# Fixed places for the factors, an earlier norm and a fourth activation tile in a two-layer trunk

## The chip, the cores and the metric

The kernel runs on one core of a Trainium2 chip. A core has five engines with a queue each, which run independently and wait for each other by semaphores: TensorE (PE, matrix products into PSUM; PEld is its loading of weights), VectorE (DVE), ScalarE (ACT), GpSimd (POOL, which can't reach PSUM) and SyncE (SP, which here issues loads). The metric is the device time of one execution in microseconds (us), as a median of several runs.

## What is computed

One inference step of two layers on 1056 tokens (1024 of a prompt, 32 of a running stream) with 1024 features, in float32. Layer 0 mixes tokens with a gated linear recurrence (HGRN2), layer 1 with a short causal convolution; after each comes an MLP.

```
for i in range(DEPTH):                       # DEPTH = 2
    a = rmsnorm(h, norm_mix[i])
    y = hgrn2_mixer(a, ...) if i == 0 else short_conv_mixer(a, ...)
    h = h + y
    m = rmsnorm(h, norm_mlp[i])
    h = h + jnp.square(jax.nn.relu(m @ w_up[i])) @ w_down[i]   # 1024 -> 4096 -> 1024
return rmsnorm(h, norm_final), states
```

## The kernel before

Activations lie transposed: a tile is 128 features by 1056 tokens, and `hT` are the eight tiles of `h`. Each float32 product is made of three matmuls of rounded operands: the low half of the weight by the high half of the activation, high by low, and high by high. A split (`part`, lines 597 to 604) is an ACT cast (the high half) and a DVE subtraction (the low half).

An MLP (`mlp`, line 844) goes through the 4096 hidden features in 16 chunks of 256. `up(c)` makes a chunk's two hidden tiles `u`, `sums(c)` turns them into seven factors, and `down(c, 0)` and `down(c, 1)` multiply these into the two halves of `hT`. Both products use a scheme of Strassen's kind: sums of blocks of the weights (made on GpSimd, line 756) times factors of the activations, which are named B11, B22, Q1, Q2, T3, B21 and T4 (`xsums`, line 765, in which the sums overwrite `u` in place).

A `down` has seven steps of 12 matmuls (`STEPS`, line 744), 84 in all, that read B11, Q1, Q2, B22, T3, B21 and T4 in this order. After each step its result is added to `hT`: by DVE (line 915), or, for the first and the last step, by an ACT copy into a tile `st` (two buffers, line 912) and a GpSimd add (line 913). An `up` has eleven products (`PAIR`, line 811): seven with a factor, of 12 matmuls each, and four with plain rows of the input, of 24 each, 180 matmuls in all. Products with the same letter there add up in the same PSUM tile; one that is read in between must be read before the next adds to it. The first `up` of an MLP takes them in the order `LATE` (line 814) and calls `nrm.scale` ahead of product 10, which is the tenth in that order; `scale` (line 701) spreads the sum of squares with matmuls (line 707) and computes 1/rms on DVE in a chain of whole-tile operations (lines 143 to 149). The ends of the first `up` (relu, times 1/rms, square) run after its products.

The stages follow in the text as up(0), sums(0), up(1), down(0,0), down(0,1), sums(1), up(2), down(1,0), down(1,1), and so on. The weights of a stage are loaded and split two stages ahead in the text. Factors, norm tiles and others share one rotation of seven buffers (`zt`, line 627); `u` tiles have three (`ut`, line 630); a weight's halves have six buffers each (`wb`, line 619); PSUM has four tiles of two banks (`pb`, line 622).

No order is written by hand here. A scheduler at compile time simulates the program and puts into each engine's queue, of the instructions that are ready in its simulation, the one that stands first in the text. A tile that takes over a buffer waits for the readers of the one before. On the chip each queue then goes strictly in order. Pools opened after others are closed lie over the closed ones' memory: at line 619 those of the HGRN stage have just been closed, with `fp` (activations) ahead of `ws` (weights).

Of the kernel before, what the change touches and what calls it, by code (L numbers as in the profile page):

```python
# [16 lines left out]
P = 128  # L17
D = 1024
KT = D // P
NTOK = 1056  # L20
# [15 lines left out]
def trunk_kernel(  # L36
# [579 lines left out]
    fp_cm.__exit__(None, None, None)  # L616


    wb = ctx.enter_context(tc.tile_pool(name="wb", bufs=6, reuse_waits="tile"))
    hb = ctx.enter_context(tc.tile_pool(name="hb", bufs=1, reuse_waits="tile"))  # L620
    mp = ctx.enter_context(tc.tile_pool(name="mp", bufs=1, reuse_waits="tile"))
    pb = ctx.enter_context(tc.tile_pool(name="pb", bufs=4, space=PSUM, reuse_waits="tile"))

    def ht(name):
        return hb.tile([P, NTOK], F32, tag="h", name=name, bufs=8)

    def zt(name, dtype=F32):
        return hb.tile([P, NTOK], dtype, tag="z", name=name, bufs=7)

    def ut(name, dtype=F32):  # L630
        return hb.tile([P, NTOK + 4], dtype, tag="u", name=name, bufs=3)[:, :NTOK]

    work["dg"] = ut

# [77 lines left out]

    def out_proj(W, first, xsrc, vcol):

        nrm = Norm(zt)
        X = None
        for m in range(KT):
            wt = wrow(W[m])
            if first:
                hT[m] = ht(f"hT{m}")  # L720
                nc.gpsimd.dma_start(out=hT[m], in_=x_t[m * P : (m + 1) * P, :])
            _, pss = trio()
            mm_groups(pss, wt, xsrc, m in (0, KT - 1))
            for g in range(3):
                sl, n = gsl(g)
                nc.vector.tensor_tensor(hT[m][:, sl], hT[m][:, sl], pss[g][:, :n], op=ALU.add)
            nrm.add(m)
            if m in (3, 5):
                X = hsums(m // 2 - 1, X, vcol)
        X["rows"] = [parts(hT[k], vec[:, vcol + k : vcol + k + 1]) for k in range(4, KT)]  # L730
        return nrm, X
# [56 lines left out]

    def hsums(q, X, vcol):

        t = [zt("hs") for j in range(2)]
        for j in range(2):
            m = 2 * q + j
            nc.scalar.activation(t[j], hT[m], AF.Copy, scale=vec[:, vcol + m : vcol + m + 1])
        new = xt if q else lambda f: xt(f) if f == "T4" else et(f, F32R)
        Y = xsums(*t, new)
        return {f: (X[f] if X else []) + [Y[f]] for f in Y}
# [46 lines left out]
    def mlp(layer, nrm, on_final, last, X):  # L844
# [3 lines left out]
        def up(c):  # L848
            def run(w):
                u = [ut("u") for j in range(2)]  # L850
                left = {b: list(READ.values()).count(b) for b in READ.values()}
                made = set()

                def read(what, ps):
                    i, h = b = READ[what]
                    sl = slice(h * HALF, (h + 1) * HALF)
                    d = u[i][:, sl]
                    op0 = ALU.min if i else ALU.max
                    left[b] -= 1
                    src = d  # L860
                    if b in made:
                        nc.vector.tensor_tensor(q2(d), q2(d), ps, op=ALU.add)
                    elif left[b] or c == 0:
                        nc.scalar.copy(q2(d), ps)
                    else:
                        src = ps
                    made.add(b)
                    if not left[b]:
                        r = lambda: nrm.r[:, sl]

                        def end():
                            if src is d:
                                nc.vector.scalar_tensor_tensor(d, d, 0.0, r(), op0=op0, op1=ALU.mult)
                            else:
                                nc.vector.scalar_tensor_tensor(q2(d), src, 0.0, q2(r()), op0=op0, op1=ALU.mult)
                            if c:
                                nc.scalar.activation(d, d, AF.Square)
                            else:
                                nc.vector.tensor_tensor(d, d, d, op=ALU.mult)

                        later.append(end) if c == 0 else end()

                later = []
                if c:
                    mm_pair(w, X, read)
                else:
                    mm_pair(w, X, read, LATE, {10: nrm.scale})
                for f in later:
                    f()
                U[c] = u  # L890

            return lambda: wpair(Wu[c]), run

        def sums(c):
            Z[c] = xsums(*U.pop(c), lambda f: zt(f, F32R))

        def down(c, b):
            def run(w):
                x = Z[c]
                ps = [{}, {}]  # L900
                for i, (bank, f, g, start) in enumerate(STEPS):
                    for p in range(2):
                        if start:
                            ps[p][bank] = pt()
                        t = ps[p][bank]
                        mm_half(t, w(f, p), x[g], start, True)
                        v = t[:, :, :QT]
                        r, h, op = TO[i]
                        d = hT[4 * b + 2 * p + r][:, h * HALF : (h + 1) * HALF]
                        if i in (0, 6):  # L910
                            st = mp.tile([P, HALF], F32, tag="st", name="st", bufs=2)
                            nc.scalar.copy(q2(st), v)  # L912
                            nc.gpsimd.tensor_tensor(d, d, st, op=op)  # L913
                        else:
                            nc.vector.tensor_tensor(q2(d), q2(d), v, op=op)  # L915

            return lambda: wsums(Wd[c, b]), run
# [18 lines left out]
            return lambda: wblocks(Wd[NFC - 1, b]), run  # L936

        G = []

        def gsplit(u, new):  # L940
            h, l = [new(t, F32R) for t in ("gh", "gl")]
# [46 lines left out]
        stages.append(up(n))  # L988
        if last:
            stages += [down(n - 1, 0), down(n - 1, 1)]  # L990
            stages.append(lambda: [gsplit(u, zt) for u in U[n]])
            stages.append(up(n + 1))
            stages.append(lambda: [gsplit(U[n + 1][0], zt), gsplit(U[n + 1][1], lambda t, d: (zt if t == "gh" else ut)(t, d))])
            stages.append(groups())
        else:
            stages.append(down(n - 1, 0))
# [24 lines left out]
    with tc.tile_pool(name="cv", bufs=1) as cv:  # L1021
# [2 lines left out]
        ys = []  # L1024
        for m in range(KT):
            wts = [wrow(wg_cu_conv[2 * m + j]) for j in range(2)]
            z = hb.tile([P, NTOK + 4], F32, tag="u", name="z", bufs=3)
            zp = lambda g: [(z[:, 2 + GROUPS[g][0] : 2 + min(NPR, sum(GROUPS[g]))], 0, min(NPR, sum(GROUPS[g])) - GROUPS[g][0])] + (
                [(z[:, NPR + 4 : NTOK + 4], NPR - GROUPS[g][0], NTOK - GROUPS[g][0])] if g == 2 else [])
            nc.gpsimd.memset(z[:, 0:2], 0.0)  # L1030
# [28 lines left out]
            nc.scalar.activation(ct, z[:, 0:L], AF.Copy, scale=w(0))  # L1059
            nc.vector.scalar_tensor_tensor(ct, z[:, 1 : 1 + L], w(1), ct, op0=ALU.mult, op1=ALU.add)  # L1060
            nc.vector.scalar_tensor_tensor(ct, z[:, 2 : 2 + L], w(2), ct, op0=ALU.mult, op1=ALU.add)
            y = (zt if m < 7 else ut)(f"y{m}")
            nc.vector.tensor_tensor(y[:, :NPR], ct[:, :NPR], r[:, :NPR], op=ALU.mult)
            nc.vector.tensor_tensor(y[:, NPR:], ct[:, NPR + 2 :], r[:, NPR:], op=ALU.mult)
            ys.append(y)
# [15 lines left out]
    def fin1(g, m):  # L1081
# [20 lines left out]
        if (g, m) == (2, KT - 1):  # L1102
            final_scale(g)
            for k0 in range(0, KT, 2):
                o = zt("o")[:, : 2 * n].rearrange("p (k c) -> p k c", k=2)
                for k in range(2):
                    final_mul(g, k0 + k, nc.gpsimd if k0 + k in (2, 5) else nc.vector, o[:, k])
                nc.sync.dma_start(out=y_t[k0 * P : (k0 + 2) * P, sl].rearrange("(k p) c -> p k c", p=P), in_=o)
# [109 lines left out]
```

## Time and profile before

| what | value |
|---|---|
| median of 3 runs | 2489.42 us (2489.13 to 2491.89) |
| profiled execution | 2489.7 us |
| its span, first to last instruction | 2488.0 us |
| mean granted TensorE clock | 0.988 |
| busy: PE, DVE, ACT, POOL | 96%, 71%, 37%, 32% |

Times in rows are microseconds from the span's start. Where a row ends in square brackets, the engine was idle for that long before the instruction, until the named releaser was done. Layer 0's MLP runs from about 628 to 1370, layer 1's from about 1735 to 2488.

### The profile page before, as it was taken

The page shows a single profiled execution, that of the slowest core. Times are in us where ns is not written, and L with a number is a line of the kernel's source. Part 1 is how long each engine was busy: PE and PEld are TensorE (multiplying, and loading weights), DVE is VectorE, ACT ScalarE, POOL GpSimd, SP SyncE. Part 2 cuts the span into 40 slices and gives each one's busy share as a digit, 9 for nine tenths or more (in the row PEclk, how much of TensorE's full clock was granted, in tenths as well). Part 3 has the DMA queues.
Part 4 walks back from the last instruction along what each step waited for, and adds up shares of the span by engine and source line. Part 5 has one row for each costly group of instructions (what it writes and reads, how often), then busy time and mean ns, then how long its engine had stood idle before and what let it go on. Part 6 is the DMA issues. An engine that isn't in the chain of part 4 may idle for free. (4 is left out here: it accounts for less than half of the span.)

```text
span 2488.0 us, 42845 instructions
## 1 busy us (share of the span) xinstructions
PE 2392.9 (96%) x17700; PEld 2339.4 (94%) x17700; DVE 1769.9 (71%) x2842; ACT 917.8 (37%) x1671; POOL 792.2 (32%) x920
## 2 busy tenths in 40 slices
PE   8999999979799999999999999999899999999998
PEld 8999999979799999999999999999799999999997
DVE  8775757553888788887888633345888887888865
ACT  5121212133344444444445111134244444444444
POOL 2110101002245454444545000002254544545433
PEclk9999999989899999999999999999899999999999
DMA  4101010031011111111111111110111111111111
GB/s 148 38 30 46 24 52 21 13 123 43 26 52 52 43 43 52 52 52 44 43 52 52 51 43 51 43 45 33 35 52 43 52 52 43 52 43 52 52 52 70
DMA packets 35779, 122.23 MB, mean 49 GB/s; under 512 B 4336, under 2 KB 7552, under 8 KB 35584
## 3 DMA queue, kind: packets, MB, share of 16 engines
q1 hardware_dynamic: 33632, 113.58, 14.4%
q0 software_dynamic: 1952, 5.92, 0.6%
q8 instruction: 139, 2.28, 0.4%
q14 instruction: 56, 0.46, 0.1%
HBM read 114.09 MB, written 5.39 MB: 48 GB/s over the span
## 5 line engine op out<-in xcount | busy, mean ns | idle before, releaser
L600 ACT CAST whi<-raw 128x512 fp32r<-128x512 f32 (+1 forms) x476 | 275.9, 580 | 756.3 <-PE pb L117 290.9
L756 POOL TENSOR_TENSOR raw<-raw 128x256 f32<-128x256 f32 x360 | 307.1, 853 | 538.5 <-DVE wlo L601 523.8
L601 DVE TENSOR_TENSOR wlo<-raw,whi 128x512 fp32r<-128x512 f32 (+1 forms) x476 | 327.9, 690 | 142.3 <-ACT whi L600 140.6
L915 DVE TENSOR_TENSOR hT<-hT,pb 128x528 f32<-128x528 f32 x580 | 389.4, 697 | 54.2 <-PE pb L806 49.1
L913 POOL TENSOR_TENSOR hT<-hT,st 128x528 f32<-128x528 f32 x232 | 339.4, 1474 | 194.4 <-ACT st L912 194.4
L806 PE MATMUL pb<-B,whi 128*128 128x264 f32 x2160 | 353.9, 286 | 5.5 <-DVE B L601 5.5
L115 PE MATMUL pb<-xh,wlo 128*128 128x384 f32 (+1 forms) x960 | 312.4, 325 | 9.3 <-DVE wlo L601 9.3
L117 PE MATMUL pb<-xh,whi 128*128 128x384 f32 (+1 forms) x960 | 311.0, 324 | 0.0
L116 PE MATMUL pb<-xl,whi 128*128 128x384 f32 (+1 forms) x960 | 309.9, 323 | 0.8 <-DVE xl L604 0.8
L806 PEld LDWEIGHTS pb<-B,whi 128*128 128x128 f32 x2160 | 301.7, 190 | 5.9 <-DVE B L601 5.9
L806 PE MATMUL pb<-B,wlo 128*128 128x264 f32 x1080 | 224.4, 289 | 41.0 <-DVE hT L915 21.7
L806 PE MATMUL pb<-T,whi 128*128 128x264 f32 x1440 | 234.8, 285 | 0.0
L806 PE MATMUL pb<-Q,whi 128*128 128x264 f32 x1440 | 233.8, 284 | 0.0
L806 PEld LDWEIGHTS pb<-B,wlo 128*128 128x128 f32 x1080 | 168.4, 190 | 48.4 <-DVE hT L915 28.0
L806 PE MATMUL pb<-xh,wlo 128*128 128x264 f32 x1024 | 210.1, 286 | 0.0
L806 PE MATMUL pb<-xh,whi 128*128 128x264 f32 x1024 | 209.1, 285 | 0.0
L806 PE MATMUL pb<-xl,whi 128*128 128x264 f32 x1024 | 208.6, 285 | 0.0
L806 PEld LDWEIGHTS pb<-T,whi 128*128 128x128 f32 x1440 | 200.3, 189 | 0.0
L806 PEld LDWEIGHTS pb<-Q,whi 128*128 128x128 f32 x1440 | 199.2, 188 | 0.0
L115 PEld LDWEIGHTS pb<-xh,wlo 128*128 128x128 f32 x960 | 181.1, 189 | 9.7 <-DVE wlo L601 9.4
L115 PE MATMUL pj<-xh,wlo 128*128 128x384 f32 (+1 forms) x536 | 176.6, 330 | 6.5 <-ACT xh L192 6.5
L116 PEld LDWEIGHTS pb<-xl,whi 128*128 128x128 f32 x960 | 180.9, 188 | 1.2 <-DVE xl L604 1.2
(265 smaller groups left out, 4875.7 us busy)
## 6 DMA issues: line engine op xcount, KB each, us to landing
raw<-in_wg_up_dram SPq DMA_DIRECT2D x64, 512.0 KB, 3.5
raw<-in_wg_down_dram SPq DMA_DIRECT2D x64, 512.0 KB, 3.5
raw<-in_wg_in_hgrn_dram SPq DMA_DIRECT2D x31, 512.0 KB, 4.0
raw<-in_wg_cu_conv_dram SPq DMA_DIRECT2D x16, 512.0 KB, 3.6
xk<-in_x_t_dram SPq DMA_DIRECT2D x8, 528.0 KB, 8.3
hT<-in_x_t_dram POOLq DMA_DIRECT2D x8, 528.0 KB, 9.3
raw<-in_wg_out_hgrn_dram SPq DMA_DIRECT2D x8, 512.0 KB, 4.9
raw<-in_wg_b_conv_dram SPq DMA_DIRECT2D x8, 512.0 KB, 3.6
```

The source lines that it names most:

```text
L115: nc.tensor.matmul(ps, wlo, ah, start=start, stop=False)
L116: nc.tensor.matmul(ps, whi, al, start=False, stop=False)
L117: nc.tensor.matmul(ps, whi, ah, start=False, stop=stop)
L600: nc.scalar.copy(h, src)
L601: nc.vector.tensor_tensor(l, src, h.bitcast(F32), op=ALU.subtract)
L756: nc.gpsimd.tensor_tensor(t(d), t(d), t(o), op=ALU.add)
L806: nc.tensor.matmul(ps[:, q, :QT], w, half(v, q), start=start and n == 0, stop=stop and n == 2, skip_group_check=True)
L913: nc.gpsimd.tensor_tensor(d, d, st, op=op)
L915: nc.vector.tensor_tensor(q2(d), q2(d), v, op=op)
```

## The change

The factors of a chunk no longer rotate. Each has a fixed place, a buffer of its own, and takes in the next chunk the place that another factor had (`AFTER`): B11 that of T4, T4 that of B11, B22 that of B21, B21 that of T3, T3 that of Q1, Q1 that of B22; Q2 stays. Norm tiles, `hsums`, the conv stage's `y`, the last chunks' halves and the output tiles get fixed places as well. In the first `up`, `nrm.scale` is called ahead of product 2, the sixth in `LATE`, and so after five products. There are four `u` tiles, four `st` buffers and seven buffers for each weight half; the SBUF for them comes from GpSimd's DMA scratch, 4096 instead of the default 16384 bytes of a partition. The pool `hb` is opened ahead of `wb`.

```diff
-    wb = ctx.enter_context(tc.tile_pool(name="wb", bufs=6, reuse_waits="tile"))
     hb = ctx.enter_context(tc.tile_pool(name="hb", bufs=1, reuse_waits="tile"))
+    wb = ctx.enter_context(tc.tile_pool(name="wb", bufs=7, reuse_waits="tile"))
...
-    def zt(name, dtype=F32):
-        return hb.tile([P, NTOK], dtype, tag="z", name=name, bufs=7)
+    def zt(i, name, dtype=F32):
+        return hb.tile([P, NTOK], dtype, tag=f"z{i}", name=name, bufs=1)

     def ut(name, dtype=F32):
-        return hb.tile([P, NTOK + 4], dtype, tag="u", name=name, bufs=3)[:, :NTOK]
+        return hb.tile([P, NTOK + 4], dtype, tag="u", name=name, bufs=4)[:, :NTOK]
...
-        nrm = Norm(zt)
+        sqs = iter((0, 1, 2, 1, 2, 1, 2, 1, 2))
+        nrm = Norm(lambda name: zt(next(sqs), name))
...
-        t = [zt("hs") for j in range(2)]
+        t = [zt(3 + 2 * q + j, "hs") for j in range(2)]
...
-                    mm_pair(w, X, read, LATE, {10: nrm.scale})
+                    mm_pair(w, X, read, LATE, {2: nrm.scale})
...
+        AFTER = {"B11": "T4", "B22": "B21", "B21": "T3", "Q1": "B22", "Q2": "Q2", "T3": "Q1", "T4": "B11"}
+        place = {f: i for i, f in enumerate(AFTER)}
+
         def sums(c):
-            Z[c] = xsums(*U.pop(c), lambda f: zt(f, F32R))
+            Z[c] = xsums(*U.pop(c), lambda f: zt(place[f], f, F32R))
+            place.update({f: place[AFTER[f]] for f in AFTER})
...
-                            st = mp.tile([P, HALF], F32, tag="st", name="st", bufs=2)
+                            st = mp.tile([P, HALF], F32, tag="st", name="st", bufs=4)
...
+        gi = iter(range(8))
+
+        def gz(name, dtype):
+            i = next(gi)
+            return zt(i, name, dtype) if i < 7 else ut(name, dtype)
...
-            z = hb.tile([P, NTOK + 4], F32, tag="u", name="z", bufs=3)
+            z = hb.tile([P, NTOK + 4], F32, tag="u", name="z", bufs=4)
...
-            y = (zt if m < 7 else ut)(f"y{m}")
+            y = zt(m, f"y{m}") if m < 7 else ut(f"y{m}")
...
-                o = zt("o")[:, : 2 * n].rearrange("p (k c) -> p k c", k=2)
+                o = zt(k0 // 2, "o")[:, : 2 * n].rearrange("p (k c) -> p k c", k=2)
...
-    nc = _bacc.Bacc("TRN2", target_bir_lowering=False, num_devices=1)
+    nc = _bacc.Bacc("TRN2", target_bir_lowering=False, num_devices=1, dynamic_dma_scratch_size=4096)
```

## Rows read from the trace of the kernel before

**Rows 1.** The page's first part: busy time, share of the span, instructions.
```profile
PE 2392.9 (96%) x17700; PEld 2339.4 (94%) x17700; DVE 1769.9 (71%) x2842; ACT 917.8 (37%) x1671; POOL 792.2 (32%) x920
```

**Rows 2.** PE's waits, whole span: waiter <- releaser: us in total, times, longest.
```profile
PE pb L806 <- DVE hT L915: 31.1, 57, 1.8
PE pb L806 <- ACT u L864: 21.0, 4, 9.5
PE pb L115 <- DVE wlo L601: 9.3, 1, 9.3
```

**Rows 3.** Busy us by stretch: one chunk's first `down`, second `down`, and an `up`.
```profile
1044.37:1054.59 10.22, 10.22 (x86) 10.22 (x85) 8.66 (x14) 4.38 (x8) 5.45 (x6) 1.00 0.08 30
1054.59:1066.80 12.21, 11.20 (x87) 10.48 (x86) 10.53 (x16) 5.76 (x11) 8.95 (x9) 1.00 0.19 51
1022.45:1044.37 21.92, 21.92 (x182) 21.92 (x181) 17.24 (x25) 10.32 (x18) 6.90 (x6) 1.00 0.19 56
```
The columns of this view are the stretch, its length, the busy time of PE, PEld, DVE, ACT and POOL with their instructions, the granted clock, the DMA share and GB/s.

**Rows 4.** PE's waits in the steady stretches 700 to 1300 and 1800 to 2360.
```profile
PE pb L806 <- DVE hT L915: 14.4, 28, 0.8
...
PE pb L806 <- DVE hT L915: 13.3, 26, 0.8
```

**Rows 5.** In order of time, a second `down`: ACT, then DVE (start, us, instruction).
```profile
1057.62 0.60 ACT L912 COPY st<-pb 128x528 f32<-128x528 f32 x1 [0.87 <-POOL hT L913]
1058.12 1.17 ACT L600 CAST B<-u 128x528 fp32r<-128x528 f32 x2
...
1057.00 0.70 DVE L915 TENSOR_TENSOR hT<-hT,pb 128x528 f32<-128x528 f32 x1 [0.60 <-PE pb L806]
1058.79 1.34 DVE L601 TENSOR_TENSOR B<-u,B 128x528 fp32r<-128x528 f32 x1 [1.08 <-ACT B L600]
1060.06 2.53 DVE L915 TENSOR_TENSOR hT<-hT,pb 128x528 f32<-128x528 f32 x4
```

**Rows 6.** Busy us by stretch: `up(1)` from first to last matmul, layers 0 and 1.
```profile
653.23:690.47 37.24, 25.01 (x188) 24.49 (x187) 31.65 (x40) 11.87 (x20) 8.48 (x5) 0.82 0.09 27
1759.92:1798.32 38.40, 26.21 (x188) 25.69 (x187) 31.64 (x40) 11.85 (x20) 8.47 (x5) 0.78 0.09 28
```

**Rows 7.** In order of time, the start of layer 0's MLP: POOL, PE, DVE, ACT.
```profile
632.62 3.03 POOL L698 TENSOR_TENSOR acc<-acc,sq 128x1056 f32<-128x1056 f32 x1 [12.41 <-ACT sq L697]
...
645.36 1.29 PE L707 MATMUL pb<-acc,ones 128*128 128x384 f32 x4
...
646.87 0.91 DVE L708 TENSOR_SCALAR nv<-pb 128x384 f32<-128x384 f32 x2
...
669.54 1.22 PE L806 MATMUL pb<-B,whi 128*128 128x264 f32 x4 [2.76 <-DVE B L601]
...
679.61 0.58 ACT L864 COPY u<-pb 128x528 f32<-128x528 f32 x1
...
679.74 0.71 DVE L604 SCALAR_TENSOR_TENSOR T<-u,T 128x528 fp32r<-128x528 f32 x1 [0.71 <-ACT T L603]
...
680.24 0.81 PE L806 MATMUL pb<-B,wlo 128*128 128x264 f32 x2 [9.47 <-ACT u L864]
```

**Rows 8.** SyncE's waits in 510 to 548.
```profile
SPq L654 <- DVE xl L601: 89.6, 1, 89.6
```

**Rows 9.** In order of time, the start of `out_proj`: DVE and POOL.
```profile
523.73 4.74 DVE L601 TENSOR_TENSOR xl<-Y,xh 128x1056 fp32r<-128x1056 f32 x4
531.95 1.29 DVE L601 TENSOR_TENSOR wlo<-raw,whi 128x512 fp32r<-128x512 f32 x2 [3.48 <-ACT whi L600]
...
524.10 1.07 POOL L721 DMA_DIRECT2D hT<-in_x_t_dram  x2 [0.52 <-issue]
```

**Rows 10.** PE's waits in 2360 to 2412, the end of layer 1's `down` stages.
```profile
PE pb L806 <- DVE hT L915: 2.4, 2, 1.8
```

**Rows 11.** DVE's groups in one chunk (1022.45 to 1066.8): count, busy us, mean ns, idle before.
```profile
L601 DVE TENSOR_TENSOR B<-u,B 128x528 fp32r<-128x528 f32 x3 | 3.9, 1291 | 1.1 <-ACT B L600 1.1
L775 DVE TENSOR_TENSOR u<-u 128x528 f32<-128x528 f32 x4 | 2.8, 707 | 0.1
```

More of the change, by code (lines that the diff above doesn't have):

```diff
@@ L990, in mlp @@
             stages += [down(n - 1, 0), down(n - 1, 1)]
-            stages.append(lambda: [gsplit(u, zt) for u in U[n]])
+            stages.append(lambda: [gsplit(u, gz) for u in U[n]])
             stages.append(up(n + 1))
-            stages.append(lambda: [gsplit(U[n + 1][0], zt), gsplit(U[n + 1][1], lambda t, d: (zt if t == "gh" else ut)(t, d))])
+            stages.append(lambda: [gsplit(u, gz) for u in U[n + 1]])
             stages.append(groups())
```

## The prediction

> **What bounds the kernel now.** I read four views, in this order. The page's first part says that TensorE (PE) is the bound: matmuls are busy 96% of the span [rows 1]. A gain can therefore only come from PE's remaining waits, and the list of PE's waits, longest first, is short: 31.1 us in 57 waits for the DVE add of line 915, 21.0 us in 4 waits for the ACT copy of line 864, and one wait of 9.3 us for a weight half [rows 2]. The third view, busy time by stretch, shows what they cost inside one chunk of an MLP: `up` takes 21.92 us and the first `down` 10.22 us with PE busy throughout, while the second `down`, with the same 84 matmuls, takes 12.21 us [rows 3]. One matmul costs 10.22 / 84 = 0.1217 us in the undisturbed stages, so the second `down` loses 1.99 us. The list of PE's waits over the steady part of each layer gives the count: 28 waits in layer 0 and 26 in layer 1, two for each chunk, so 27 chunks [rows 4]. The waits alone are (14.4 + 13.3) / 27 = 1.03 us a chunk; the rest of the 1.99 us is restarts after them, too short for the list. The fourth view, the instructions in order of time, tells why.
>
> **Part 1, the steady chunk.** In the second `down`, PE reads the old factor B11 first. As soon as it has, ACT may write the new B11 into the same buffer, and DVE's low half of it stands in DVE's queue among the evictions. ACT comes late: its copy into `st` at 1057.62 waits 0.87 us for GpSimd's add, because there are two `st` buffers, and the cast of B follows only at 1058.12. DVE sits 1.08 us on that cast, then needs 1.34 us, and four evictions run back to back behind it from 1060.06 [rows 5]. PE waits for those. The change takes away both causes. B11 goes to the place of T4, which PE reads last in the stage, and B22 to that of B21, read next to last: neither can be written before the evictions in question are out. Four `st` buffers take away ACT's wait for GpSimd. What it adds: 1.34 us of DVE work moves into the next `up`, where DVE is busy 17.24 of 21.92 us [rows 3], so it fits; ACT's cast of B11 now waits for the last T4 matmul, and behind it in ACT's queue stand only weight casts and the first read of `up`, which PE needs no sooner than its fifth product, 60 x 0.1217 = 7.3 us into the stage. The sums then end about a microsecond later than now, and the next `down` needs them only at the end of `up`. The second `down` keeps 10.53 - 1.34 = 9.19 us of DVE work for 10.22 us, near the 8.66 us with which the first `down` loses nothing [rows 3]. The seventh weight buffer may pull one more weight half (1.29 / 2 = 0.65 us [rows 9]) into it, which would bring DVE to 9.8 of 10.2 us. So the bubble's return is bounded by nothing left and by half of it left (1.0 us); I take 0.2 us, nearer the first `down`'s row. Gain: 27 x (1.99 - 0.2) = 48.3, say 48 us; between 27 and 53.7 us.
>
> **Part 2, the start of each MLP.** From the first matmul of `up(1)` to the last, 37.24 us go by in layer 0 and 38.40 us in layer 1 [rows 6]. PE has 180 + 6 matmuls in it (one half-step of `down(0,0)` was slipped in): 186 x 0.1217 = 22.6 us. So 14.6 and 15.8 us are lost, 30.4 us in all. In order of time [rows 7]: the matmuls that spread the sum of squares run at 645.36, after 132 of `up(0)`'s 180 matmuls; DVE starts the 1/rms at 646.87 and has the last factor, T4, at 679.74 + 0.71 = 680.45, almost without a pause. `up(1)` cannot run meanwhile, since there are three `u` tiles and its second one waits until the sums are through with `up(0)`'s first: ACT's copy into it comes at 679.61, and PE, which waits 2.76 us for B11's low half and then 9.47 us for that copy, goes on at 680.24. The granted clock over the stretch is 0.82 [rows 6], that is, part of it at the 1.2 GHz level after the pause. The fourth `u` tile ends the wait for the copy outright. Moving `nrm.scale` from the tenth to the sixth product of `LATE` brings it forward by 72 matmuls, 72 x 0.1217 = 8.8 us; the sum of squares is complete at 632.62 + 3.03 = 635.65, and 645.36 - 8.8 = 636.6 is just after. DVE's chain then starts at about 638 and needs its 33.6 us, plus at most the 646.87 - 638 = 8.9 us of other work that it does now before the chain: T4 between 671.6 and 680.5. PE would reach the end of `up(1)` at 653.23 + 21.94 = 675.2, needs the first factor then and T4 only 72 matmuls later, at 684. So the factors are in time, T4 by 3.5 us or more. What is late next: `up(1)`'s own evictions, which stand behind the sums in DVE's queue, and bank `c`, which in `up(0)` must now wait for the trio of banks that `scale` takes. Neither shows in the trace; I bound them by nothing and by two waits like the 2.76 us above, 5.5 us a layer, and take 1.2 us, nearest to the 1.03 us that PE waits for an eviction in a chunk. Gain 30.4 - 2.4 = 28 us, between 19.4 and 30.4.
>
> **Part 3, the pool order and the rest.** The first weights of `out_proj` lie where the HGRN stage's tiles lay, and SyncE's load of them waits for one of the last `xl` of line 601 [rows 8]; the weight's low half follows at 531.95 and PE waits 9.3 us for it [rows 2, 9]. With the activations first, the weights come to lie over the old weight pool, free earlier. But DVE is busy with `xl` until 523.73 + 4.74 = 528.47 [rows 9], and the weight's low half is behind those in the text. So PE starts some 531.95 - 528.47 = 3.5 us sooner, not 9.3. The other bound is a loss: the `hT` loads, issued from 524.10 now, may have to wait for those same last `xl`, 4.4 us. I take 3.5 us, the row of DVE's queue. Near the end of layer 1 the same bubble as in part 1 comes with 2.4 us of waits [rows 10]; I take 1.7. The fixed places of norm and output tiles, the smaller DMA scratch (eight loads from GpSimd, each needed a tile's matmuls apart) and the two extra `st` buffers add no instruction; PE's work covers them, and if that cover fails it is the loss bounded above.
>
> Sum: 48 + 28 + 3.5 + 1.7 = 81.2 us off the profiled execution's 2489.7 us (span 2488.0 us), which stands 0.3 us above the median: 2408 us.
>
> **Rivals.** (a) The bubble half returns: DVE's queue gets a weight half instead of B11. Then 27 x 0.8 = 22 us of the 48 go: 2430 us. For it: 9.8 of 10.2 us. Against: the first `down` runs without loss on a queue nearly as full. (b) The starts stay, because the scheduler again slips something in that PE waits for: 2408 + 28 = 2436 us. Against: the one wait of 9.47 us has one cause, the third `u` tile. (c) The bubble stays whole, since PE's wait is for a PSUM bank and `pb` keeps its four tiles: only parts 2 and 3 count, 2489.7 - 33 = 2457 us. For it: the wait is for line 915, which empties a bank [rows 4]. Against: the first `down`, with the same four tiles, has none. The Trainium skill ("Perfetto Trace Analysis", Optimization Strategy) says that the same gap repeating on the engine that should be saturated can mean too little SBUF or PSUM for the next tile; by that rule, read for PSUM, this is where the change would end, and the trace's answer is the first `down`. (d) Slower: the sums, moved whole into `up`, collide with GpSimd. The casts' low halves of B take 1291 ns on average in a chunk, against 707 ns for the adds of line 775 [rows 11], so some DVE work is stretched beside GpSimd. If all of GpSimd's 6.90 us in `up` were added to DVE's 17.24 + 1.34, DVE would need 25.5 us, 3.6 us more than PE's 21.92 [rows 3]: 27 x (3.6 - 1.99) = 43 us lost, less 33 us gained elsewhere, 2500 us. It decides from 21.92 - 18.58 = 3.3 us of stretching on, and `up` as it stands holds two of the three B halves already. The skill ("SBUF — State Buffer", Who interferes with whom) says of a DVE operation and a GpSimd operation on their shared port that whichever issues second waits for the whole of the other; that is the mechanism of this rival, and the adds at 707 ns show that most of the sums don't meet it. (e) Nothing changes: the waits named are replaced one for one; about 2489 us.
>
> **How the numbers follow.** Forecast 2408 us with 0.68; (a) 0.12, (b) 0.06, (c) 0.07, (d) 0.04, (e) 0.03. By its bounds the forecast's own span is 2489.7 - (53.7 + 30.4 + 9.3 + 2.4) = 2394 us to 2489.7 - (27 + 19.4 - 4.4 + 0) = 2448 us. The range 2393 to 2442 us leaves out (c), (d), (e) and the tail of the forecast, 2 in 10. About 0.2% (5 us) is what a measurement of this kernel can tell from no change; faster by more than that is everything but (d) and (e): 0.93, within it 0.03, slower 0.04.
>
> **What would show it.** Right: in the new profile both `down` stages take 10.2 to 10.5 us and the waits for line 915 fall from 57 to a few; no wait for line 864 above 2 us; `up(1)` of each layer is 22 to 24 us long; the B halves lie in `up`; PE's wait at the start of `out_proj` is 5 to 6 us. Wrong: waits for line 915 in other places of the chunk, DVE above 21 us in `up`, or a new wait for the banks of `scale` in `up(0)`. The step I am least sure of is the order that the compile-time scheduler gives the queues, which no row of before shows for the changed program.

## The result and the profile after

The changed kernel takes 2497.78 us (median of 8 runs, 2497.03 to 2499.47) against 2489.61 us of the kernel before on the same chip: 1.0032 times as long, 95% interval 1.0021 to 1.0043. It is slower by 0.32%, where 2408 us had been forecast. Its profiled span is 2495.6 us, 7.6 us more than before, at the same mean granted clock of 0.988. PE's busy time is nearly that of [rows 1], so the time is again a matter of its waits:

```profile
PE 2395.5 (96%) x17700; PEld 2345.9 (94%) x17700; DVE 1747.7 (70%) x2842; ACT 917.1 (37%) x1671; POOL 848.7 (34%) x920
```

Where the time went, by the stretches of PE's own instructions in the two profiled executions (us):

| stretch | before | after | forecast | measured |
|---|---|---|---|---|
| up to layer 0's first `up` matmul | 627.37 | 623.67 | -3.5 | -3.7 |
| up(0), layers 0 and 1 | 25.86, 25.96 | 30.57, 31.41 | 0 | +10.2 |
| up(1), layers 0 and 1 | 37.24, 38.40 | 27.63, 27.81 | -28 | -20.2 |
| end of up(1) to the layer's last `down`, 0 and 1 | 643.04, 622.97 | 655.69, 632.20 | -49.7 | +21.9 |

The sum is +8.2 us; the remaining -0.6 us of the span lies outside these stretches. So half of the gain in up(1) was lost again one stage earlier (the two first `up` stages together take 58.2 and 59.2 us instead of 63.1 and 64.4), and the steady chunks, where most of the gain was forecast, became longer. The list of PE's waits over the whole span, to be held against [rows 2], names both:

```profile
PE pb L807 <- ACT st L918: 42.3, 28, 1.5
PE pb L707 <- POOL acc L698: 10.4, 2, 5.2
PE pb L807 <- DVE hT L921: 7.9, 29, 0.3
...
PE pb L115 <- DVE wlo L601: 5.8, 1, 5.8
```

(Lines are shifted by the edit: 806 is now 807, 864 is 865, 912 to 915 are 918 to 921.) The 31.1 us of waits for the DVE eviction fell to 7.9 and the 21.0 us for the copy of line 864 to 0.9, as forecast. In their place stand 28 waits of 1.5 us for the ACT copy into `st`, one in each steady second `down`, and two of 5.2 us for the sum of squares. One chunk by stage (stretch, length, busy PE, PEld, DVE, ACT, POOL, granted clock, DMA share, GB/s): an `up`, a first `down`, a second `down`, and the second `down` of another chunk:

```profile
1021.48:1043.52 22.04, 22.04 (x180) 22.04 (x181) 17.53 (x26) 10.45 (x19) 11.02 (x9) 1.00 0.17 55
1043.52:1053.75 10.23, 10.23 (x86) 10.23 (x85) 9.37 (x15) 4.45 (x8) 4.11 (x4) 1.00 0.17 50
1053.75:1066.47 12.72, 10.93 (x86) 10.32 (x84) 8.52 (x15) 5.56 (x11) 8.42 (x8) 1.00 0.12 33
781.35:795.42 14.07, 12.29 (x86) 11.86 (x85) 9.39 (x15) 5.42 (x11) 8.40 (x8) 0.88 0.14 42
```

Against [rows 3] the first `down` is unchanged and the second one went from 12.21 to 12.72 us, though DVE has 2 us less to do in it (8.52 instead of 10.53; the prediction had worked out 1.34 us less). DVE's work was not what PE now waited for. The same second `down` in order of time, in the changed kernel, from 1053 to 1061: ACT, POOL, DVE, PE:

```profile
1053.21 1.34 ACT L918 COPY st<-pb 128x528 f32<-128x528 f32 x2 [0.32 <-PE pb L807]
1054.73 0.60 ACT L918 COPY st<-pb 128x528 f32<-128x528 f32 x1 [0.18 <-PE pb L807]
1057.92 0.62 ACT L600 CAST whi<-raw 128x512 fp32r<-128x512 f32 x1 [2.58 <-POOL raw L757]
1058.44 0.59 ACT L918 COPY st<-pb 128x528 f32<-128x528 f32 x1
...
1055.17 0.76 POOL L757 TENSOR_TENSOR raw<-raw 128x256 f32<-128x256 f32 x1
1055.86 1.34 POOL L919 TENSOR_TENSOR hT<-hT,st 128x528 f32<-128x528 f32 x1
1057.14 0.74 POOL L757 TENSOR_TENSOR raw<-raw 128x256 f32<-128x256 f32 x1
...
1058.57 1.12 DVE L601 TENSOR_TENSOR wlo<-raw,whi 128x512 fp32r<-128x512 f32 x1 [4.20 <-ACT whi L600]
1059.61 2.53 DVE L921 TENSOR_TENSOR hT<-hT,pb 128x528 f32<-128x528 f32 x4
...
1059.09 0.51 PE L807 MATMUL pb<-Q,wlo 128*128 128x264 f32 x2 [1.51 <-ACT st L918]
```

A weight is cast twice, as loaded and after GpSimd has made its block sums (line 757). Here the cast of a block sum stands in ACT's queue ahead of the last of these copies into `st`. It needs the second sum, which ends at 1057.88, because GpSimd takes its sums (0.75 us) in turns with the adds of line 919 (1.34 us). ACT stands still for 2.58 us with the copy behind it; DVE stands still for 4.20 us, because the low half of the same weight is next in its queue, with four evictions behind that. PE, out of PSUM tiles, waits for the copy. That is the theory for the steady chunk; the experiments test it.

### The profile page after: what moved, and what is told of

Same layout as the page of the kernel before. It is cut to its first block, busy times and chain, and to the rows that moved or that the text cites. A ratio compares the mean times of both kernels' runs of the same rounds, so it can differ in the third digit from the quotient of the medians.

```text
span 2495.6 us, 42858 instructions
## 1 busy us (share of the span) xinstructions
PE 2395.5 (96%) x17700; PEld 2345.9 (94%) x17700; DVE 1747.7 (70%) x2842; ACT 917.1 (37%) x1671; POOL 848.7 (34%) x920
## 4 chain that ended last, share of the span: by engine, by line
PE 74%; POOL 8%; issue 8%; DVE 8%; ACT 2%; DMA 0%; DVEq 0%; SPq 0%; POOLq 0%; ACTq 0%
PE pb L807 34%; PE pb L115 6%; PE pb L117 6%; PE pb L116 6%; POOL hT L919 6%; PE pj L115 4%; PE pj L116 3%; PE pj L117 3%; DVE wlo L601 2%; POOL raw L757 2%; PE v L501 1%; PE v L503 1%; PE v L502 1%; PE aps L394 1%; ACT whi L600 1%
## 5 line engine op out<-in xcount | busy, mean ns | idle before, releaser
L757 POOL TENSOR_TENSOR raw<-raw 128x256 f32<-128x256 f32 x360 | 371.4, 1032 | 365.5 <-DVE wlo L601 237.7
L601 DVE TENSOR_TENSOR wlo<-raw,whi 128x512 fp32r<-128x512 f32 (+1 forms) x476 | 362.4, 763 | 186.7 <-ACT whi L600 180.9
L919 POOL TENSOR_TENSOR hT<-hT,st 128x528 f32<-128x528 f32 x232 | 329.4, 1431 | 335.9 <-ACT st L918 335.9
L807 PE MATMUL pb<-Q,wlo 128*128 128x264 f32 x720 | 150.9, 291 | 42.3 <-ACT st L918 42.3
```

The source lines that it names most:

```text
L601: nc.vector.tensor_tensor(l, src, h.bitcast(F32), op=ALU.subtract)
L757: nc.gpsimd.tensor_tensor(t(d), t(d), t(o), op=ALU.add)
L807: nc.tensor.matmul(ps[:, q, :QT], w, half(v, q), start=start and n == 0, stop=stop and n == 2, skip_group_check=True)
```

## The experiments

A time without a range is that of a single run.

### Six weight buffers instead of seven

```diff
-    wb = ctx.enter_context(tc.tile_pool(name="wb", bufs=7, reuse_waits="tile"))
+    wb = ctx.enter_context(tc.tile_pool(name="wb", bufs=6, reuse_waits="tile"))
```

> The changed kernel with six instead of seven buffers for each weight half, all else as changed. Weight-buffer theory: the seventh buffer lets a weight cast that waits for GpSimd's block sums enter ACT's queue between two copies into st, and PE's new wait (28 times 1.51 us for the ACT copy of line 918) comes from that. Then those waits go, a steady chunk falls from 45.0 us (46.2 us in the chunks in which the clock falls) to 42.4 to 43.0 us, and the kernel to 2425 to 2440 us. Rival, st theory: the four st buffers let GpSimd's adds crowd out its block sums; then the chunk stays at 45 us and the kernel at about 2497 us. Rival, place theory: B11's new place empties the slot in the queues and something else fills it whatever the buffers; then the chunk stays at 44.3 us or above.

Measured: 2442.78 us (2442.30 to 2443.27), 0.9808 of the kernel before, interval 0.9793 to 0.9822. The wait for `st` is gone, as the weight-buffer theory has it, and both its rivals fall; the chunk takes 43.2 us, and chunk and time are a little above the theory's ranges. First PE's waits in this kernel, then its second `down` by the columns above, then ACT, DVE and PE in order of time in that stretch:

```profile
PE pb L807 <- DVE hT L921: 15.1, 29, 1.0
...
952.33:963.26 10.93, 10.41 (x87) 10.20 (x85) 9.24 (x15) 4.73 (x10) 8.65 (x8) 1.00 0.16 49
...
952.84 1.81 ACT L918 COPY st<-pb 128x528 f32<-128x528 f32 x3
958.43 0.62 ACT L600 CAST whi<-raw 128x512 fp32r<-128x512 f32 x1 [3.78 <-DVE hT L921]
961.25 0.62 ACT L600 CAST whi<-raw 128x512 fp32r<-128x512 f32 x1 [2.19 <-POOL raw L757]
...
961.90 0.69 DVE L601 TENSOR_TENSOR wlo<-raw,whi 128x512 fp32r<-128x512 f32 x1 [0.87 <-ACT whi L600]
```

ACT's cast still waits for GpSimd, here 2.19 us, but the copies into `st` are through long before it, and DVE has its evictions ahead of the weight half; the second `down` loses 0.7 us instead of 2.5. So the seventh buffer alone turned a gain of 48 us into a loss of 8. What it alters is the order in which the compile-time scheduler queues ACT's casts and copies. That it does so because a buffer free earlier makes the cast ready earlier in the scheduler's simulation is argued, not shown.

### The seventh buffer alone on the kernel before

```diff
-    wb = ctx.enter_context(tc.tile_pool(name="wb", bufs=6, reuse_waits="tile"))
+    wb = ctx.enter_context(tc.tile_pool(name="wb", bufs=7, reuse_waits="tile"))
...
+    dynamic_dma_scratch_size=4096
```

> The kernel before with seven buffers for each weight half (and the smaller scratch that makes room for them), nothing else changed. Weight-buffer theory: the seventh buffer alone makes the new wait. Then PE waits 1.3 us or more for the ACT copy into st in every chunk, the chunk goes from 44.3 us to 45 us or more, and the kernel to 2505 us or more. Rival (the seventh buffer harms only together with the other parts, because they move the sums away): the chunk stays at 44.3 us within 0.2 us, the kernel within 5 us of the kernel before.

Measured: 2530.57 us against 2491.18 us, 39 us slower; the chunk is 45.6 us. PE's waits show the same new wait, so neither the fixed places nor the norm are needed for it:

```profile
PE pb L806 <- ACT st L912: 43.4, 28, 1.6
```

The seventh buffer also lengthens the first `up`, from 25.9 and 26.0 us to 31.2 and 30.0.

### Two rival causes of the new wait: four `st` buffers, the exchange of places

With two `st` buffers in the changed kernel (`bufs=4` to `bufs=2`):

> The changed kernel with two instead of four st buffers. St theory: the 28 waits of 1.51 us go and the chunk falls to 43 us or less. Weight-buffer theory: the weight cast still stands between the copies, the waits stay at 1.3 us or more, and the chunk at 44.8 us or above; about 2497 us or more.

And with every factor in a place of its own throughout, `AFTER` being the identity:

> The changed kernel with each factor always in its own place (B11 in B11's, and so on), seven weight buffers. Place theory: the wait for the ACT copy of line 918 goes and the old bubble of the kernel before (waits for line 921's add, 0.8 us, chunk 44.3 us) comes back. Weight-buffer theory: the ACT waits of 1.5 us stay, and B11's cast adds to them: chunk 45 us or more.

Measured: 2501.93 and 2507.0 us; the waits of PE for `st` are 43.6 us in 28 and 42.0 us in 28. Both rivals fall: the wait has neither cause. The exchange of places, which loses 9 us here when taken out, does not show its worth beside this wait.

### GpSimd's block sums: left out, put aside, put aside but late

First the sums are left out:

```diff
-        for d, o in ((2, 3), (3, 0), (0, 2), (1, 0)):
-            nc.gpsimd.tensor_tensor(t(d), t(d), t(o), op=ALU.add)
```

> The changed kernel, seven weight buffers, with GpSimd's four sums of weight blocks left out of every Strassen stage (so its products are of wrong blocks; this only times). Weight-buffer theory: the weight cast between the copies into st is harmful because it waits for those sums, behind GpSimd's adds. Without them it has nothing to wait for, PE's waits for the ACT copy into st go, and the chunk falls from 45.0 us to 42.4 to 43.0 us. Rival (the cast's own 0.62 us on ACT and the low half on DVE are what is too much in the second down): the chunk stays at 44 us or more, and waits for ACT's copy remain.

Measured: 2409.01 us, chunk 42.4 us, which is 348 matmuls of 0.1217 us without a gap. The two `down` stages and the `up` between 931.99 and 974.40:

```profile
931.99:942.21 10.22, 10.22 (x86) 10.22 (x85) 9.06 (x15) 4.38 (x8) 2.62 (x2) 1.00 0.16 50
942.21:952.45 10.24, 10.24 (x86) 10.24 (x85) 9.49 (x14) 5.27 (x11) 5.62 (x4) 1.00 0.17 52
952.45:974.40 21.95, 21.95 (x183) 21.95 (x181) 17.54 (x26) 10.51 (x19) 3.08 (x2) 1.00 0.16 50
```

DVE has 9.49 us to do in the second `down` and PE loses nothing, which is what the prediction had said of DVE. But leaving the sums out takes away GpSimd's work as well as the cast's wait. So next they are made, into a tile nobody reads:

```diff
-            nc.gpsimd.tensor_tensor(t(d), t(d), t(o), op=ALU.add)
+            nc.gpsimd.tensor_tensor(mp.tile([P, 256], F32, tag="sj", name="sj", bufs=1), t(d), t(o), op=ALU.add)
...
-                            st = mp.tile([P, HALF], F32, tag="st", name="st", bufs=4)
+                            st = mp.tile([P, HALF], F32, tag="st", name="st", bufs=3)
```

> The changed kernel with seven buffers for the weight halves, but GpSimd's four block sums of every weight tile go to a small tile of their own that nobody reads (a third of the st room is given for it, three buffers instead of four). So GpSimd does the same adds as in the changed kernel, but no weight cast waits for them (the block sums are missing from the result). Theory, the harm comes from the cast that waits for GpSimd in ACT's queue: time as without the sums, 2405 to 2420 us, chunk 42.4 to 42.6, no wait of PE for the ACT copy into st. Rival, the harm comes from GpSimd's adds themselves, which run beside DVE and ACT and stretch them: the chunk stays above 43 us and the time above 2435 us.

Measured: 2547.15 us against 2490.56. The theory's time is missed by far, and the rival's bounds hold (chunk 47.0 us, above 43; time above 2435 us), but not at the place in question: the wait for `st` is gone, both `down` stages are without loss (10.23 and 10.26 us), and the loss is in `up`, 26.91 instead of 22 us. In order of time there: POOL, DVE, PE:

```profile
1087.55 7.96 POOL L757 TENSOR_TENSOR sj<-raw 128x256 f32<-128x256 f32 x7
...
1088.07 1.25 DVE L776 TENSOR_TENSOR u<-u 128x528 f32<-128x528 f32 x1
...
1096.00 0.70 DVE L776 TENSOR_TENSOR u<-u 128x528 f32<-128x528 f32 x1
...
1097.91 0.51 PE L807 MATMUL pb<-T,wlo 128*128 128x264 f32 x2 [3.19 <-ACT u L865]
```

No longer held back by the casts, seven sums run in one row beside DVE's sums, and the same DVE operation takes 1.25 us until 1095.51, where that row ends, and 0.70 us after it. This is the mechanism of rival (d), brought about by the experiment itself: it could not answer its question, since it moved GpSimd's work. The Trainium skill ("SBUF — State Buffer", Who interferes with whom) names a shared port pair of DVE and GpSimd that one of them locks; these rows agree as far as both are slower beside each other, GpSimd's sum with 7.96 / 7 = 1.14 us instead of 0.75. Which of them gives way differs: in a steady `up` of the changed kernel four sums run beside DVE's sums as well, and there it is GpSimd's that take longer, 6.42 / 4 = 1.6 us each, while DVE's adds of line 776 stay at 0.70 us:

```profile
1029.08 6.42 POOL L757 TENSOR_TENSOR raw<-raw 128x256 f32<-128x256 f32 x4 [4.11 <-issue]
```

What decides it was not tried. So the last kernel holds the sums back to where they were, by reading the weight's low half, which is made after the first cast:

```diff
+            low = hl[1][1] if d > 1 else hl[0][1][:, d * 256 : (d + 1) * 256]
-            nc.gpsimd.tensor_tensor(mp.tile([P, 256], F32, tag="sj", name="sj", bufs=1), t(d), t(o), op=ALU.add)
+            nc.gpsimd.tensor_tensor(mp.tile([P, 256], F32, tag="sj", name="sj", bufs=1), t(d), low.bitcast(F32), op=ALU.add)
```

> Like the run before it, the four block sums go to a small tile that nobody reads (so they are missing from the result), three st buffers; but each sum now reads the low half of its weight in place of the second block, so GpSimd can begin it no sooner than in the changed kernel, and eight of the twelve stand in one row behind each other in its queue, as there. Theory, the cast that waits for GpSimd in ACT's queue does the harm: 2405 to 2425 us, chunk 42.4 to 42.8, no wait of PE of a microsecond that repeats by chunk. Rival, GpSimd's adds stretch what runs beside them on DVE: the additions of line 776 and the low halves of B, Q and T take 1.2 us instead of 0.7 over much of `up`, the chunk stays above 44 us and the time above 2470 us, with the wait in `up` and not in the second `down`.

Measured: 2429.54 us against 2491.09; the chunk is 42.9 us on average, both a little above the expectation of the theory. A first `down`, a second one and an `up`:

```profile
937.72:947.95 10.23, 10.23 (x86) 10.19 (x85) 9.21 (x14) 4.38 (x8) 4.28 (x4) 1.00 0.13 36
947.95:958.65 10.70, 10.60 (x87) 10.37 (x85) 10.11 (x15) 5.72 (x12) 9.03 (x8) 1.00 0.17 59
958.65:980.70 22.05, 22.05 (x181) 22.05 (x181) 17.46 (x26) 10.29 (x19) 11.16 (x9) 1.00 0.16 52
```

GpSimd is busy for 24.47 us in these three stages (23.55 in the changed kernel), no wait of PE above 0.2 us recurs by chunk, and with seven buffers the time is 68 us below that of the changed kernel. So the cast that waits for GpSimd is the larger part, and GpSimd's adds as a neighbour the smaller. By the loss of the second `down` against 10.22 us: 2.5 us in the changed kernel, where the cast waits and stands ahead of a copy; 0.7 us with six buffers, where it waits nearly as long (2.19 us) but stands behind the copies; 0.5 us here, where it stands behind them too and doesn't wait; none without GpSimd's sums. The place in the queue is thus worth 1.8 us, given that the cast waits. Whether the wait would cost less if the place were kept was not tried apart: with the wait gone, the scheduler also puts the cast behind the copies. The last 0.5 us, with DVE busy for 10.11 instead of 9.49 us, goes with GpSimd's adds beside it.

### What the other parts are worth, on six buffers

Six buffers, and `AFTER` the identity:

> Six weight buffers, every other part as changed, but each factor always in its own place. Place theory (B11 in T4's place is what empties the second down of the sums): B11's cast stands in the second down again, its waits for the DVE add come back, and a steady chunk goes from 43.2 us to 43.8 to 44.5 us; the kernel from 2443 us to 2460 to 2480 us. Rival, st theory (four st buffers let ACT cast B11 in time, and the place is of no account): the chunk stays at 43.2 us within 0.2 us.

Measured: 2476.5 us, chunk 44.36 us, second `down` 12.23 us, all as the place theory expects, and PE waits for the DVE add. But this is not the old wait. In the kernel before, PE waits 0.8 us in a chunk ahead of the fourth step (B22) and 0.2 us ahead of the last (T4); here it waits once, 1.7 us, ahead of the last. The waits over the whole span, then ACT, DVE and PE late in the second `down` from 959.97 to 972.20:

```profile
PE pb L807 <- DVE hT L921: 47.3, 29, 1.8
...
969.35 1.14 ACT L600 CAST whi<-raw 128x512 fp32r<-128x512 f32 x2 [2.11 <-POOL raw L757]
970.00 0.69 DVE L601 TENSOR_TENSOR wlo<-raw,whi 128x512 fp32r<-128x512 f32 x1 [1.49 <-ACT whi L600]
971.36 0.51 PE L807 MATMUL pb<-T,wlo 128*128 128x264 f32 x2 [1.71 <-DVE hT L921]
```

Again a cast waits for a block sum, DVE's low half waits for the cast, and the evictions stand behind it. B11's cast is back in the second `down`, but 2.2 us after its start instead of 3.5 (1058.12 less 1054.59, [rows 3, 5]), and without a wait for GpSimd's add.

So the exchange of places is worth 2476.5 - 2442.8 = 34 us, 1.2 us a chunk; that it is worth this by ending the old wait is not shown. Six buffers, and two `st`:

> Six weight buffers, factors in the new places, two st buffers instead of four. Place theory: nothing of weight stands behind the copies into st any more, so the chunk stays at 43.2 us within 0.3 us and the kernel at 2440 to 2450 us. St theory: ACT waits for GpSimd's adds again, PE's wait of 0.8 us in the second down comes back, and the chunk goes to 43.8 us or more (2460 us or more).

Measured: 2443.25 us, chunk 43.1 to 43.3 us. The four `st` buffers are worth nothing here, with the exchange in. Two `st` buffers without the exchange were not tried on six buffers, so whether the four are what ended the old wait in the run above stays open. Six buffers, and three `u` tiles:

> Six weight buffers, the other parts as changed, but three u tiles. If the fourth u tile is what shortens up(1), PE's wait for the ACT copy into u comes back in both layers (6 to 9.5 us each), up(1) with its 6 slipped matmuls goes from 28.1 us to 34 to 38 us, and the kernel from 2443 us to 2455 to 2465 us; the steady chunk stays at 43.2 us. Rival (the earlier norm alone shortens it): up(1) stays at 28 to 30 us and the kernel within 4 us of 2443 us.

Measured: 2445.92 us, so the fourth `u` tile is worth about 3 us, not the 12 or more expected. With it missing, PE waits again for ACT's copy into `u`, but 4.8 us at most instead of 9.5 [rows 2], and with four tiles it waits 3.8 and 3.9 us for DVE's eviction in the same stage:

```profile
PE pb L807 <- ACT u L865: 9.5, 2, 4.8
```

up(1) with its six extra matmuls takes 29.15 us in layer 0, 28.11 with four tiles, 37.24 in the kernel before. That is not the earlier norm's work alone, since up(0) is 5 us longer in both than before: up(0) and up(1) together take 60.1 and 58.9 us in layer 0, 63.1 before.

### When the norm is called

In the changed kernel, back ahead of product 10 (`{2: nrm.scale}` to `{10: nrm.scale}`):

> The changed kernel with the norm called ahead of product 10 as in the kernel before, seven weight buffers. Norm-timing theory: called five products in, the spreading matmuls come to stand after 24 of the first up's matmuls, before the sum of squares is complete, and PE waits 5.2 us in each layer; with the call at product 10 these two waits go, the first up falls from 30.6 and 31.4 us to 25.9 us, and as up(1) has a free u tile, it stays at 22 to 27 us: the kernel gains 5 to 10 us, 2488 to 2493 us. Rival: the later norm delays the sums and the first down waits for its factors by as much as was gained; then the kernel stays at 2497 us.

Measured: 2500.21 us (2499.57 to 2501.46), no gain, as the rival expects. The wait for `acc` is gone, up(0) takes 29.9 and 30.0 us, up(1) 31.5 and 31.8, and PE waits for the first `Q` factor and, in up(0), for an eviction instead:

```profile
PE pb L807 <- ACT Q L600: 9.7, 2, 4.9
...
PE pb L807 <- DVE u L863: 6.5, 4, 2.6
```

The wait of 2.6 us in up(0) is not the norm's: the kernel before with seven buffers has it too (2.5 us), at the same place. So with seven buffers up(0) is 30 to 31 us long with either place of the call.

With six buffers and the call ahead of product 8:

> Six weight buffers, the other parts as changed, the norm called ahead of product 8, eight products in, where the spreading matmuls stand after 108 of the first up's 180 matmuls instead of after 24. Norm-timing theory: the sum of squares is complete by then, so the two waits of 5.2 us go and the first up falls from 30.8 us to 25 to 27 us; the sums start some 6 us later than with five products, and the first down waits for its factors or the banks for about as much. If the waits only move, first up and up(1) together stay at 58.9 us within 1.5 us and the kernel at 2443 us; if the earlier norm is what matters, they rise by 2 to 4 us a layer; if the wait was pure loss, they fall by 3 to 5 us a layer.

Measured: 2439.4 us (2438.7 to 2441.41), 0.9794 of the kernel before, interval 0.9778 to 0.981: the fastest of the kernels that compute the whole result. up(0) is 26.4 us in both layers, up(1) 31.5 and 31.3; together 57.9 and 57.8, where six buffers with the call ahead of product 2 need 58.9 and 60.2, the changed kernel 58.2 and 59.2, the kernel before 63.1 and 64.4. So the waits mostly move: with the early call PE waits 5.2 us for `acc` and 3.8 for an eviction in layer 0, with the later one 4.3 us for the first `Q` factor and 1.7 for its low half.

### Five weight buffers

`bufs=5`, and the call ahead of product 8:

> Five weight buffers, the norm ahead of product 8, the other parts as changed. The six-buffer kernel still loses 0.8 us a chunk, to a weight half at the start of up whose cast waits for GpSimd's sums. Weight-buffer theory: with one buffer fewer that cast moves on by one place too, and the chunk falls to 42.4 to 43.0 us, the kernel to 2418 to 2435 us. Rival: five buffers are too few, weights come late and PE waits for weight halves (waits of the matmuls for the low halves of line 601): chunk 43.5 us or more, the kernel above 2445 us.

Measured: 2511.64 us (2510.64 to 2512.37), 1.0089 of the kernel before, interval 1.0072 to 1.0106; chunk 45.3 us, as the rival expects. PE waits at three places of a chunk, one of them for a weight half:

```profile
PE pb L807 <- ACT st L918: 15.3, 27, 0.6
PE pb L807 <- DVE wlo L601: 14.8, 28, 0.7
...
PE pb L807 <- DVE hT L921: 12.5, 31, 1.3
```

Five and six buffers with this call give 2511.6 and 2439.4 us, six and seven with the call of the change 2442.8 and 2497.8 us: six is the best of the three, and the two sides fail in different ways.

## Why the prediction was wrong

**Part 1, the steady chunk, the step that failed.** The reading of the old bubble fits its rows: the cast and the low half of B stood ahead of the evictions [rows 5], and PE waited behind them:

```profile
1060.80 0.52 PE L806 MATMUL pb<-B,wlo 128*128 128x264 f32 x2 [0.80 <-DVE hT L915]
```

The exchange of places takes them out of the second `down` and is worth 34 us with six buffers. But the run without it doesn't test this reading, as its wait is another one, behind the cast of a block sum. DVE's 9.5 us in a second `down` cost PE nothing when nothing waits. What failed is the sentence on the seventh buffer, "may pull one more weight half", priced at 0.65 us of DVE's work and bounded by half of the old bubble. The buffer's price was not the work of the extra half but its wait: 2.58 us of ACT's queue, 4.20 us of DVE's, with the evictions behind it. The bound held for work, and a queue that stands still on another engine has no such bound: 12.72 us, above even the old 12.21. The prediction asked what is queued behind ACT's cast of B11 and answered for that cast alone; the casts of block sums wait for GpSimd, and the list of ACT's waits in the kernel before had shown it:

```profile
ACT whi L600 <- POOL raw L756: 98.5, 87, 2.9
```

PE's list names none of these 87 waits [rows 2]. In the changed kernel ACT waits less in all for these sums (83.1 us, 34 times); what changed is where such a wait stands in the queue, and it costs PE 2.5 us or more in each second `down`. **The `st` buffers**: ACT's 0.87 us for GpSimd was real, but four buffers instead of two are worth nothing with the exchange in; whether they would have been enough without it was not tried.

**Part 2, the starts: one step of the mechanism wrong, sizes wrong.** Forecast 28 us, measured 10.0: 20.2 us gained in up(1), 10.2 us lost in up(0). First, the spreading matmuls were to come 72 matmuls earlier, after 60. In the changed kernel they come after 24, since the compile-time scheduler put them ahead of products 4, 7 and 6, and they wait for the sum of squares. PE and POOL in order of time, layer 0:

```profile
631.94 1.65 PE L707 MATMUL pb<-acc,ones 128*128 128x384 f32 x2 [5.20 <-POOL acc L698]
...
628.89 3.00 POOL L698 TENSOR_TENSOR acc<-acc,sq 128x1056 f32<-128x1056 f32 x1 [12.40 <-ACT sq L697]
```

The prediction had placed them at 636.6 and `acc` at 635.65, "just after"; with everything 3.7 us earlier, `acc` came at 631.9 as reckoned, and PE stood at the wait since 626.74. Nor did the factors come much sooner: counted from up(0)'s first matmul, B11's low half begins at 41.4 us before and 41.5 us after, and T4 is done at 53.1 and 52.0. Second, up(1) was to take 22 to 24 us. "`up(1)`'s own evictions, which stand behind the sums in DVE's queue" were rightly named as what is late next, and the wait for them is 1.88 + 0.54 us in layer 0, inside the bound of 5.5 us; but what follows it, a restart at the lower clock, was left out. The two first `up` stages of layer 0 by the columns above, then up(1) in the kernel without GpSimd's sums:

```profile
623.67:654.24 30.57, 25.37 (x188) 24.18 (x187) 25.67 (x30) 11.38 (x16) 6.28 (x5) 0.94 0.14 46
654.24:681.87 27.63, 24.80 (x189) 24.19 (x187) 25.50 (x36) 11.43 (x20) 7.11 (x7) 0.94 0.07 22
...
655.25:678.21 22.96, 22.90 (x188) 22.69 (x187) 22.02 (x35) 11.71 (x20) 2.06 (x1) 1.00 0.07 24
```

The granted clock of up(1) is 0.94, up from 0.82 [rows 6] but not 1.00, and that of up(0) is 0.94 too, behind the wait that the change put there. Without the sums up(1) has the length that was forecast. In the changed kernel four of them run beside DVE's work ahead of the evictions, which goes on without a pause and takes 2.2 us longer for it. POOL, DVE and PE in the changed kernel, then the same DVE work without the sums:

```profile
661.30 4.57 POOL L757 TENSOR_TENSOR raw<-raw 128x256 f32<-128x256 f32 x4 [18.90 <-DVE wlo L601]
662.87 2.40 DVE L880 TENSOR_TENSOR u<-u 128x528 f32<-128x528 f32 x2
675.20 0.48 PE L807 MATMUL pb<-B,wlo 128*128 128x264 f32 x2 [1.88 <-DVE u L863]
...
662.23 1.32 DVE L878 TENSOR_TENSOR u<-u 128x528 f32<-128x528 f32 x2
```

Third, the fourth `u` tile did end the wait for the copy, from 9.5 to 0.5 us at most, but with six buffers and the early call that is worth 3 us, as PE then waits for an eviction. How much of the 10.0 us each part brought can't be told apart: with seven buffers and the old call, the other parts together shorten the two stages from 68.8 to 61.3 us in layer 0, and the early call from there to 58.2.

**Part 3 was right**: PE's wait at the start of `out_proj` fell from 9.3 [rows 2] to 5.8 us, and layer 0's first `up` begins 3.7 us sooner, for 3.5 forecast. **The end of layer 1** came out in size: its last such second `down` fell from 14.53 to 12.73 us, 1.8 for 1.7 forecast. That is partly luck, since the new wait of 1.5 us stands in it and the old ones of 2.4 us [rows 10] are gone.

**The rivals.** None was what happened as a whole. (a) and (c), a bubble that comes back half or whole, had the size of the bubble but not its cause, and neither let it grow. Beside (c) stood the rule of the Trainium skill ("Perfetto Trace Analysis", Optimization Strategy) that a repeating gap can mean too little memory; here one buffer fewer (five) and one more (seven) both made a repeating gap. (d) did not occur in the steady `up` of the changed kernel, where the adds of line 776 stay at 0.70 us; its mechanism occurred in up(1), by the rows above, and where an experiment moved GpSimd's sums. (b), the scheduler slipping something in at the starts, did occur, in up(0), and took half of the gain in up(1). The chance of 0.04 for slower was too small because every rival but (d) kept PE's new waits below the old ones, while the step called least sure, the order that the scheduler gives the queues, got no rival with a price of its own.

## What to carry to other kernels

Before adding a buffer to a pool whose order a compile-time scheduler decides, list the waits of the engines that are not the bound: a wait there that costs nothing today (87 waits of up to 2.9 us) can become a cost under a new order (here 2.5 us a chunk), and the size of the queue's work does not bound it. Try such a count one step to either side, since here one buffer fewer than six cost 72 us and one more 55. Measure two stages together when a change can move a wait from one to the other. And bring the parts of a change in one by one: the exchange of places, worth 34 us, was hidden by a buffer that cost 55.

## What the chip showed that was not expected

A wait of 1.5 us costs more in some chunks than in others: of the 28 second `down` stages of the changed kernel that have it, 21 take 12.7 us and seven 14.1. In one of the latter, the granted clock after the wait that ends at 786.69 (two stretches of 3 us):

```profile
786.00:789.00 3.00, 2.04 (x13) 1.83 (x14) 2.83 (x4) 0.64 (x2) 2.92 (x4) 0.94 0.00 0
789.00:792.00 3.00, 3.00 (x16) 3.00 (x16) 2.88 (x6) 0.62 (x1) 0.98 (x1) 0.50 0.00 0
```

Behind the wait the clock falls to 0.50, the 1.2 GHz level, in the three microseconds of the second row, in which PE does 16 matmuls instead of 25; in the chunk shown first it stays at 1.00 after the same wait. What tells the two apart was not tried.
